# One queue for the first transfers of a decoder step, a shorter TensorE warm-up, and GpSimd on part of the last multiply

## The chip, the cores and the metric

The kernel runs on one core of one Trainium2 chip. The metric is the device time of one execution in microseconds (us). The kernel before was timed in three runs on the chip, and one further execution was taken with the hardware profiler. A core has five engines that run their own instruction streams: TensorE (PE, matrix multiply, with its weight loads shown apart as PEld), VectorE (DVE), ScalarE (ACT), GpSimd (POOL) and SyncE (SP). Transfers between memory and the core are issued by SP or by ACT (shown as SPq and ACTq) and carried out by 16 DMA engines.

## The reference

It is one inference step of one layer of a hybrid decoder, on 256 prompt tokens and 8 single-token samples (T = 264 columns, model width 2048):

```python
x = x + FFN_RES * swiglu(rmsnorm(x, n1), f1g, f1u, f1d)
h = rmsnorm(x, nm)
proj = h @ w_in
o_att, k_buf, v_buf = attend(q, k, v, sinks)
o_rwkv, shift, S = rwkv_time_mix(proj[..., ATT_COLS:], ...)
x = x + mixed @ w_out
x = x + FFN_RES * swiglu(rmsnorm(x, n2), f2g, f2u, f2d)
...
y = rmsnorm(x, final_norm)
```

where `swiglu(x, wg, wu, wd) = (silu(x @ wg) * (x @ wu)) @ wd` with an inner width of 5504 and `rmsnorm` divides by the root of the mean square and multiplies by a weight per feature. All values are float32.

## The kernel before

**Layout.** Features lie on the 128 partitions, tokens along the free dimension. The activations x are 16 tiles of 128 x 264 (`KD` = 16, `T` = 264). Each product keeps float32 accuracy by splitting both operands into a high part, rounded to the type TensorE reads, and a low part, the rest. Three matmuls are then run for each pair of 128 x 128 weight block and x tile: high by high, high by low, low by high (lines 140 to 142).

**Weights.** They are never kept. `chunk` (line 116) loads four 128 x 128 blocks (256 KB, 128 x 512) into one of six `raw` buffers by a transfer on SP, ACT casts them into one of four `hi` buffers, and VectorE (or GpSimd) subtracts to get one of four `lo` buffers. `gemm` (line 129) then runs the twelve matmuls of the chunk into a PSUM bank.

**The start.** `body` lets TensorE multiply a tile of ones by itself `NWARM` times (line 157), with no use for the result. `first_ffn` (line 280) issues, all on ACT, the transfer of `vec` (156 columns of norm weights and other vectors for the whole kernel) and six transfers of x. `ffn` (line 209) begins with a first phase over the eight PSUM banks: `load` splits the first four x tiles, then for every group of four x tiles (`k0` = 0, 4, 8, 12, the four rounds) it runs one chunk into each of the eight banks in turn, the gate and up halves of four column blocks. The x tiles of the next round are split while the last four banks of a round run. `Norm.split` (line 167) makes the parts of one x tile: ACT multiplies by the norm weight of that feature (taken from `vec`) and rounds to the high part, VectorE makes the low part. After the first phase the FFN goes on column block by column block. In its second part (`pi` = 1) `early` (line 197) issues the transfers of two more constants on ACT.

**The middle.** `mixing` holds attention and the recurrent half, as generators that are advanced between chunks of the projections. It is not touched.

**The end.** In `second_ffn` (line 899), `nxt` squares each finished x tile, and makes `ys`, that tile times its final norm weight. After the last tile the sums of squares go through small matmuls (lines 922 to 924) into a 88 x 3 tile `rt`. Five multiplies into `hot` (line 925), with no use for their result, are in TensorE's stream behind these. Meanwhile ACT and VectorE take the root and the reciprocal of `rt`, and three more small matmuls (line 931) spread the factors over all partitions into the PSUM bank `rp`. Seven multiplies on VectorE (line 933) scale the 16 output tiles in groups of 1, 1, 2, 4, 4, 2, 2, and each group leaves by a transfer issued on SP and ACT in turn.

**What sets the order.** Each engine works through a fixed stream. The framework orders the streams before the run by simulating a timeline (line 1041), so that an instruction stands where the simulation finds its operands ready. Instructions passed to `keep_in_program_order` stay in the order of the code. Waits between engines are added by the framework.

Of the kernel before, what the change touches and what calls it, by code (L numbers as in the profile page):

```python
# [7 lines left out]
F32 = mybir.dt.float32  # L8
F32R = mybir.dt.float32r
AF = mybir.ActivationFunctionType  # L10
ALU = mybir.AluOpType
AX = mybir.AxisListType

P = 128
NP = 256
NB = 8
T = NP + NB
D = 2048
KD = 16
# [8 lines left out]
CH, NRAW, NHL = 4, 6, 4  # L28
NACC, NM = 3, 5
NS, NO, NY, NH, NT, NLD = 38, 8, 8, 40, 18, 6  # L30
NWARM = 14
NGM, NKR, NUV, NTT, NBT = 10, 5, 3, 2, 5
NSTEP = 2
DWAIT = (8, 8, 8, 8)
# [7 lines left out]
VG1, VGM, VG2, VGF = 0, 16, 32, 48  # L42
# [5 lines left out]
def body(tc, I, O):  # L48
    nc = tc.nc
    V, A, G, TE, SP = nc.vector, nc.scalar, nc.gpsimd, nc.tensor, nc.sync  # L50
    cnt = [0]

    def uid(s):
        cnt[0] += 1
        return f"{s}{cnt[0]}"

    def tt(e, out, a, b, op):
        return e.tensor_tensor(out=out, in0=a, in1=b, op=op)  # L58

    def stt(out, a, s, b, op0, op1):  # L60
        return V.scalar_tensor_tensor(out=out, in0=a, scalar=s, in1=b, op0=op0, op1=op1)  # L61
# [5 lines left out]
    def act(out, in_, f, **k):  # L67
        return A.activation(out=out, in_=in_, func=f, **k)  # L68

    def bc(ap, shape):  # L70
        return ap.broadcast_to(list(shape))

    def mm(out, lhsT, rhs, start=True, stop=True, **k):
        TE.matmul(out, lhsT, rhs, start=start, stop=stop, **k)  # L74
# [20 lines left out]
    with ExitStack() as ctx:  # L95
        cp = ctx.enter_context(tc.tile_pool(name="cp", bufs=1))
        sp = ctx.enter_context(tc.tile_pool(name="sp", bufs=1))
        wp = ctx.enter_context(tc.tile_pool(name="wp", bufs=1))
# [4 lines left out]
        def slot(shape=(P, T), dt=F32, tag="s"):  # L103
            return sp.tile(list(shape), dt, tag=tag, bufs={"s": NS, "o": NO, "y": NY}[tag], name=uid(tag))
# [8 lines left out]
        def mp():  # L113
            return pp.tile([P, 512], F32, tag="m", bufs=NM, name=uid("m"))

        def chunk(src, n, e, ahead=True):
            w = n * P
            with tc.high_priority() if ahead else nullcontext():
                raw = wp.tile([P, CH * P], F32, tag="raw", bufs=NRAW, name=uid("raw"))
                hi = wp.tile([P, CH * P], F32R, tag="hi", bufs=NHL, name=uid("hi"))  # L120
                lo = wp.tile([P, CH * P], F32R, tag="lo", bufs=NHL, name=uid("lo"))
                SP.dma_start(raw[:, :w], src)  # L122
                A.copy(hi[:, :w], raw[:, :w])  # L123
                tt(e, lo[:, :w], raw[:, :w], hi[:, :w].bitcast(F32), ALU.subtract)
            return hi, lo

        nch = [0]

        def gemm(ps, src, xs, step=None, rng=None, ahead=True, share=False):
            n = len(xs)  # L130
# [15 lines left out]
        vec = cp.tile([P, NVEC], F32, name="vec")  # L146
# [9 lines left out]
        warm = mp()  # L156
        for _ in range(NWARM):
            mm(warm[:, :P], ones, ones)

        def vc(i):  # L160
            return vec[:, i:i + 1]

        class Norm:
            def __init__(self, col, most=2):
                self.col, self.most, self.xs, self.sums = col, most, [], [[], []]

            def split(self, x, pin=False, tag="s"):
                g = vc(self.col + len(self.xs))
                hi, lo = slot(dt=F32R, tag=tag), slot(dt=F32R, tag=tag)
                keep = tc.keep_in_program_order if pin else lambda i: i  # L170
                keep(act(hi, x, AF.Copy, scale=g))
                keep(stt(lo, x, g, hi.bitcast(F32), ALU.mult, ALU.subtract))
                self.xs.append((hi, lo))

# [22 lines left out]
        def early(pi):  # L197
            keep = tc.keep_in_program_order
            if pi == 1:
                keep(A.dma_start(C, I["cst"]))  # L200
                keep(A.dma_start(ss, I["shs"]))

# [6 lines left out]
        def ffn(nrm, xr, gu, dn, nxt, load, begin=False, side=None):  # L209
            rstd = None  # L210
            f0 = 0
            for pi, nf in enumerate(PARTS):
                hs = [None] * nf
                late = []
                if begin:
                    early(pi)
# [61 lines left out]
                f0 += nf  # L278

        def first_ffn(n2):  # L280
            n1 = Norm(VG1)
            xr = []
            A.dma_start(vec, I["vec"])
            def load(k0):
                n1.split(xr[k0], k0 >= CH)

            def nxt(o):
                n2.split(xr[o])
                n2.square(xr[o])
                A.dma_start(xsp[o], xr[o])  # L290

            with tc.tile_pool(name="f1", bufs=1) as fp:
                cur[0] = (fp, NH)
                for q in range(4):
                    xg = fp.tile([P, 4, T], F32, tag="x", bufs=4, name=uid("x"))
                    for j in ((0, 1), (1, 2), (2, 4)) if q == 0 else ((0, 4),):
                        A.dma_start(xg[:, j[0]:j[1]], I["xT"][:, q * 4 + j[0]:q * 4 + j[1], :])
                    xr += [xg[:, j] for j in range(4)]
                ffn(n1, xr, I["gu1"], I["dn1"], nxt, load, True)

        def dec_state(fp, XD):
# [33 lines left out]
        def mixing_body(mx, n2, n3, XD):  # L335
# [545 lines left out]
            for pi, ks in enumerate(PASS):  # L881
                now = need(ks)
                drain(now, [g for g in tasks if g not in now])
                with tc.high_priority():
                    for k in ks:
                        split(k)
                for o in range(KD):
                    ps = acc()
                    gemm(ps, I["wout"][o, :, k0 * P:(k0 + len(ks)) * P], [mixed[k] for k in ks], tick, share=True)
                    with tc.high_priority():  # L890
                        tt(V, xr[o], ps[:, :T], xr[o], ALU.add)
                    if pi == len(PASS) - 1 and o < CH:
                        n3.split(xr[o], tag="y")
                for k in ks:
                    mixed[k] = None
                k0 += len(ks)
            return xr

        def second_ffn(n3, xr, XD):
            fin = Norm(VGF, 3)  # L900

            def load(k):
                if k >= CH:
                    n3.split(xr[k], True, "o" if k in NSO else "s")

            with tc.tile_pool(name="f2", bufs=1) as fp:
                cur[0] = (fp, NH)
                ys = [fp.tile([P, 4, T], F32, tag="y", bufs=4, name=uid("y")) for _ in range(4)]
                rt = fp.tile([88, 8], F32, name="rt")

                def nxt(o):
                    fin.square(xr[o])
                    if o == 0:
                        act(rt[:, 7:8], fin.sums[0][0][0:88, 0:1], AF.Sqrt)
                    act(ys[o // 4][:, o % 4], xr[o], AF.Copy, scale=vc(VGF + o))

                side = dec_state(fp, XD)
                ffn(n3, xr, I["gu2"], I["dn2"], nxt, load, False, side)
                assert next(side, side) is side
                p = fin.sums[0]  # L920
                sm, rp, hot = [mp(), mp()], mp(), mp()
                for m, q in zip(sm, p):
                    for j in range(3):
                        mm(m[0:88, j:j + 1], q[:, j * 88:j * 88 + 88], ones[:, 0:1])
                for _ in range(5):
                    mm(hot[:, :P], ones, p[1][:, :P])
                A.copy(rt[:, 3:6], sm[0][0:88, 0:3])
                tt(V, rt[:, 0:3], sm[1][0:88, 0:3], rt[:, 3:6], ALU.add)
                act(rt[:, 0:3], rt[:, 0:3], AF.Sqrt, scale=1.0 / D, bias=eps[0:88, 0:1])
                V.reciprocal(rt[:, 0:3], rt[:, 0:3])  # L930
                for j in range(3):
                    mm(rp[:, j * 88:j * 88 + 88], bc(rt[:, j:j + 1], (88, P)), C[0:88, CID:CID + 88])
                for i, (o, n) in enumerate(((0, 1), (1, 1), (2, 2), (4, 4), (8, 4), (12, 2), (14, 2))):
                    y = ys[o // 4][:, o % 4:o % 4 + n]
                    tt(V, y, y, bc(rp[:, :T].unsqueeze(1), (P, n, T)), ALU.mult)
                    (SP, A)[i % 2].dma_start(O["yT"][:, o:o + n, :], y)

        xsp = [dp.tile([P, T], F32, tag=f"xsp{o}", name=f"xsp{o}") for o in range(KD)]
        n2, n3 = Norm(VGM), Norm(VG2)
        first_ffn(n2)  # L940
        with tc.tile_pool(name="dx", bufs=1) as dx:
            XD = dx.tile([P, 8, NPAIR, NB], F32, name="XD")
            second_ffn(n3, mixing(n2, n3, XD), XD)
# [29 lines left out]
def layout(i):  # L973
    c = np.ascontiguousarray
    f4 = np.float32
    a = {"xT": c(np.concatenate([i["x_prompt"][0].T, i["x_sample"][:, 0].T], 1).reshape(KD, P, T).transpose(1, 0, 2))}
    for n in (1, 2):
        f = lambda w: w.reshape(KD, P, NF, P).transpose(2, 1, 0, 3).reshape(NF, P, D)
        a[f"gu{n}"] = c(np.stack([f(i[f"ffn{n}_w_gate"][0]), f(i[f"ffn{n}_w_up"][0])], 1))
# [14 lines left out]
    s, t = np.arange(64)[:, None], np.arange(64)[None, :]  # L994
# [50 lines left out]
```

## Time and profile before

| | us |
|---|---|
| three timed runs | 2010.73, 2009.62, 2011.49 |
| median | 2010.73 |
| profiled execution | 2008.12 |
| span of the profiled execution, first to last instruction | 2006.0 |

The profile page gives for each engine the busy time, its share of the span and the number of instructions. Timelines list a start, a duration, the engine, the line of the kernel, the operation, output and input tiles with their shapes, a count of merged instructions, and in square brackets the idle time before the first of them and what ended it. Most operations stand in small helpers, so L58, L61, L68 and L74 are the lines of `tt`, `stt`, `act` and `mm`. A float32 matmul of `ones` is recorded as two passes. Groups list count, busy time, mean duration in ns, and the idle time before them with its releasers. Windows give, for each stretch of the span, its length, the busy time of PE, PEld, DVE, ACT and POOL with instruction counts, then the granted TensorE clock as a share of the full one, the DMA engines' busy share and GB/s.

### The profile page before, as it was taken

To read this page: it belongs to the slowest core of one execution; us is meant where nothing else is said; L and a number is where in the kernel's file an instruction comes from. 1 tells how busy PE (TensorE), PEld (TensorE's weight loads), DVE (VectorE), ACT (ScalarE), POOL (GpSimd) and SP (SyncE) were. 2 spreads that over 40 slices of the span, in tenths; PEclk is the share of its full clock that TensorE was granted. 3 is DMA by queue.
4 is the path that set the end of the run, shared out by engine and by line. 5 is a ranking of instruction groups with operands and counts; after the bars stand their busy time and mean duration, and the time that the engine had idled before them with its cause. 6 is when DMAs were issued, how large, how long until landed. Compare 5 with 4: busy or idle time off the path is not lost.

```text
span 2006.0 us, 45669 instructions
## 1 busy us (share of the span) xinstructions
PE 1980.9 (99%) x17126; PEld 1947.9 (97%) x17126; DVE 1300.9 (65%) x2550; ACT 1053.8 (53%) x2089; POOL 336.6 (17%) x433
## 2 busy tenths in 40 slices
PE   9999999999999999999999999999999999999998
PEld 9999999999999999998888899999999999999998
DVE  5865555655556577688768667765666666666665
ACT  5644444444444456766555655654444444444445
POOL 0401101010010122121123553120101001010012
PEclk9999999999999999999999999999999999999999
DMA  6566666655656567555555546565666666666654
GB/s 223 176 187 196 183 193 193 183 185 174 188 178 183 181 197 222 154 151 134 145 145 144 158 141 195 174 181 177 190 186 193 181 188 195 184 192 182 195 179 145
DMA packets 228798, 358.73 MB, mean 179 GB/s; under 512 B 42568, under 2 KB 83680, under 8 KB 228576
## 3 DMA queue, kind: packets, MB, share of 16 engines
q1 hardware_dynamic: 222112, 347.28, 57.9%
q10 hardware_dynamic: 6464, 8.54, 1.3%
q8 instruction: 134, 2.20, 0.5%
q14 instruction: 88, 0.72, 0.1%
HBM read 347.58 MB, written 10.22 MB: 178 GB/s over the span
## 4 chain that ended last, share of the span: by engine, by line
PE 92%; DVE 3%; DMA 2%; ACT 1%; issue 1%; SPq 1%; POOL 0%; DVEq 0%; ACTq 0%; POOLq 0%
PE acc L74 85%; PE m L74 7%; DVE lo L58 1%; DMA sb<-Xt 0%; DVE Xt L58 0%; DVE st L58 0%; DMA TT<-sb 0%; DMA raw<-in_win 0%; DMA raw<-in_gu 0%; ACT L68 0%; ACT hi L123 0%; DVE y L58 0%; SPq L122 0%; ACT t L68 0%; DMA Xt<-sa 0%
## 5 line engine op out<-in xcount | busy, mean ns | idle before, releaser
L123 ACT CAST hi<-raw 128x512 fp32r<-128x512 f32 (+2 forms) x1304 | 779.0, 602 | 827.5 <-PE acc L74 747.4
L58 DVE TENSOR_TENSOR lo<-raw,hi 128x512 fp32r<-128x512 f32 (+1 forms) x1248 | 853.4, 688 | 542.6 <-ACT hi L123 522.5
L74 PE MATMUL acc<-s,hi 128*128 128x264 f32 x5940 | 1108.9, 286 | 1.7 <-ACT hi L123 1.2
L74 PEld LDWEIGHTS acc<-s,hi 128*128 128x128 f32 x5940 | 921.9, 188 | 7.7 <-issue 1.8
L74 PE MATMUL acc<-s,lo 128*128 128x264 f32 x2970 | 846.9, 286 | 2.8 <-DVE lo L58 2.8
L74 PEld LDWEIGHTS acc<-s,lo 128*128 128x128 f32 x2970 | 558.9, 188 | 6.2 <-DVE lo L58 3.4
L74 PE MATMUL acc<-t,hi 128*128 128x264 f32 x2752 | 503.0, 285 | 0.0
L74 PEld LDWEIGHTS acc<-t,hi 128*128 128x128 f32 x2752 | 426.5, 188 | 0.0
L74 PE MATMUL acc<-t,lo 128*128 128x264 f32 x1376 | 389.1, 285 | 0.0
L58 POOL TENSOR_TENSOR t<-t,t 128x264 f32<-128x264 f32 (+1 forms) x148 | 150.5, 1017 | 1150.1 <-ACT hi L123 781.5
L74 PEld LDWEIGHTS acc<-t,lo 128*128 128x128 f32 x1376 | 258.5, 188 | 0.1
L74 PE MATMUL acc<-y,hi 128*128 128x264 f32 x648 | 124.5, 285 | 0.0
L74 PEld LDWEIGHTS acc<-y,hi 128*128 128x128 f32 x648 | 101.0, 188 | 0.2
L74 PE MATMUL acc<-y,lo 128*128 128x264 f32 x324 | 91.9, 284 | 0.0
L58 DVE TENSOR_TENSOR t<-acc,t 128x264 f32<-128x264 f32 x156 | 67.4, 432 | 36.5 <-PE acc L74 36.3
L58 POOL TENSOR_TENSOR lo<-raw,hi 128x512 fp32r<-128x512 f32 x56 | 73.2, 1309 | 69.5 <-ACT hi L123 45.8
L58 POOL TENSOR_TENSOR o<-o,o 128x264 f32<-128x264 f32 x43 | 36.1, 841 | 189.9 <-ACT o L68 184.2
L74 PE MATMUL acc<-o,hi 128*128 128x264 f32 x324 | 63.3, 285 | 0.0
L74 PEld LDWEIGHTS acc<-y,lo 128*128 128x128 f32 x324 | 60.9, 188 | 0.0
L61 DVE SCALAR_TENSOR_TENSOR s<-acc,s 128x264 f32<-128x264 f32 x96 | 40.6, 427 | 15.9 <-PE acc L74 15.5
L74 PEld LDWEIGHTS acc<-o,hi 128*128 128x128 f32 x324 | 50.3, 188 | 0.0
L74 PE MATMUL m<-s,hi 128*128 128x264 f32 x260 | 48.7, 286 | 0.0
(239 smaller groups left out, 1345.8 us busy)
## 6 DMA issues: line engine op xcount, KB each, us to landing
raw<-in_gu SPq DMA_DIRECT2D x688, 256.0 KB, 3.4
raw<-in_dn SPq DMA_DIRECT2D x224, 256.0 KB, 2.9
raw<-in_win SPq DMA_DIRECT2D x152, 256.0 KB, 3.5
raw<-in_dn SPq DMA_DIRECT2D x160, 192.0 KB, 2.8
raw<-in_wout SPq DMA_DIRECT2D x48, 256.0 KB, 3.3
raw<-in_wout SPq DMA_DIRECT2D x32, 128.0 KB, 3.0
xsp<-x ACTq DMA_DIRECT2D x16, 132.0 KB, 3.5
s<-xsp SPq DMA_DIRECT2D x16, 132.0 KB, 4.5
```

Source lines behind the costliest of these rows:

```text
L58: return e.tensor_tensor(out=out, in0=a, in1=b, op=op)
L61: return V.scalar_tensor_tensor(out=out, in0=a, scalar=s, in1=b, op0=op0, op1=op1)
L74: TE.matmul(out, lhsT, rhs, start=start, stop=stop, **k)
L123: A.copy(hi[:, :w], raw[:, :w])
```

## The change

- The first transfers are issued on SP in one list with fixed order: the first x tile, w0 (the first chunk of weights), then x1, x2-3, w1, w2, x4-7, w3, x8-11, w4, x12-15, w5. The weights go into the buffers that the first six calls of `chunk` would have taken (`pre`), and these calls issue no transfer. ACT issues none of them.
- The 16 columns of the first norm's weights are appended to the first x tile in memory (`layout`) and on the core (`x0`, 280 columns), and `Norm` reads them there (`gain`). The transfer of `vec` moves to `early(1)`.
- The high part of x0 is made by VectorE (`ts`, a tensor_scalar multiply) instead of ACT.
- `NWARM` goes from 14 to 10, the `hot` multiplies from 5 to 4.
- The factors are also copied from PSUM into `rs` by ACT. The 16 output tiles are multiplied in ten instructions: VectorE keeps tiles 0 to 11 as 1, 1, 2, 4, 2, 2, and GpSimd multiplies tiles 12, 13, 14 and 15 one by one, reading `rs`. With the order of the list, the transfers of the GpSimd tiles and of tile 1 are issued on ACT, the others on SP.

```diff
-NWARM = 14
+NWARM = 10
...
-                raw = wp.tile([P, CH * P], F32, tag="raw", bufs=NRAW, name=uid("raw"))
+                raw = pre.pop(0) if pre else None
+                ready = raw is not None
+                if not ready:
+                    raw = wp.tile([P, CH * P], F32, tag="raw", bufs=NRAW, name=uid("raw"))
...
-                SP.dma_start(raw[:, :w], src)
+                if not ready:
+                    SP.dma_start(raw[:, :w], src)
...
-            def split(self, x, pin=False, tag="s"):
-                g = vc(self.col + len(self.xs))
+                self.gain = gain
+
+            def split(self, x, pin=False, tag="s", e=None):
+                k = len(self.xs)
+                g = vc(self.col + k) if self.gain is None else self.gain[:, k:k + 1]
...
-                keep(act(hi, x, AF.Copy, scale=g))
+                if e is None:
+                    keep(act(hi, x, AF.Copy, scale=g))
+                else:
+                    ts(e, hi, x, g, ALU.mult)
...
             if pi == 1:
+                keep(A.dma_start(vec, I["vec"]))
                 keep(A.dma_start(C, I["cst"]))
...
-            n1 = Norm(VG1)
             xr = []
-            A.dma_start(vec, I["vec"])
+
             def load(k0):
-                n1.split(xr[k0], k0 >= CH)
+                n1.split(xr[k0], k0 >= CH, e=None if k0 else V)
...
-                for q in range(4):
-                    xg = fp.tile([P, 4, T], F32, tag="x", bufs=4, name=uid("x"))
-                    for j in ((0, 1), (1, 2), (2, 4)) if q == 0 else ((0, 4),):
-                        A.dma_start(xg[:, j[0]:j[1]], I["xT"][:, q * 4 + j[0]:q * 4 + j[1], :])
-                    xr += [xg[:, j] for j in range(4)]
+                keep = tc.keep_in_program_order
+
+                def weights(i):
+                    raw = wp.tile([P, CH * P], F32, tag="raw", bufs=NRAW, name=uid("raw"))
+                    keep(SP.dma_start(raw, I["gu1"][i // 2, i % 2][:, :CH * P]))
+                    pre.append(raw)
+
+                x0 = fp.tile([P, T + KD], F32, name="x0")
+                keep(SP.dma_start(x0, I["xT"][:, :T + KD]))
+                n1 = Norm(VG1, gain=x0[:, T:])
+                xr.append(x0[:, :T])
+                weights(0)
+                for i, n in enumerate((1, 2, 4, 4, 4)):
+                    xg = fp.tile([P, n, T], F32, name=f"xg{i}")
+                    k = KD + len(xr) * T
+                    keep(SP.dma_start(xg.rearrange("p k t -> p (k t)"), I["xT"][:, k:k + n * T]))
+                    xr += [xg[:, j] for j in range(n)]
+                    for j in ((), (1, 2), (3,), (4,), (5,))[i]:
+                        weights(j)
...
-                for _ in range(5):
+                for _ in range(4):
                     mm(hot[:, :P], ones, p[1][:, :P])
...
-                for i, (o, n) in enumerate(((0, 1), (1, 1), (2, 2), (4, 4), (8, 4), (12, 2), (14, 2))):
+                rs = fp.tile([P, T], F32, name="rs")
+                A.copy(rs, rp[:, :T])
+                for i, (o, n) in enumerate(((0, 1), (1, 1), (2, 2), (12, 1), (4, 4), (13, 1), (8, 2), (14, 1), (10, 2), (15, 1))):
                     y = ys[o // 4][:, o % 4:o % 4 + n]
-                    tt(V, y, y, bc(rp[:, :T].unsqueeze(1), (P, n, T)), ALU.mult)
+                    e, r = (V, rp[:, :T]) if o < 12 else (G, rs)
+                    tt(e, y, y, bc(r.unsqueeze(1), (P, n, T)), ALU.mult)
                     (SP, A)[i % 2].dma_start(O["yT"][:, o:o + n, :], y)
...
-    a = {"xT": c(np.concatenate([i["x_prompt"][0].T, i["x_sample"][:, 0].T], 1).reshape(KD, P, T).transpose(1, 0, 2))}
+    x = np.concatenate([i["x_prompt"][0].T, i["x_sample"][:, 0].T], 1).reshape(KD, P, T).transpose(1, 0, 2)
+    a = {"xT": c(np.concatenate([x[:, 0], i["ffn1_norm"][0].reshape(KD, P).T, x[:, 1:].reshape(P, -1)], 1))}
```

More of the change, by code (lines that the diff above doesn't have):

```diff
@@ L125, in chunk @@
             return hi, lo
-        nch = [0]
+        nch, pre = [0], []
         def gemm(ps, src, xs, step=None, rng=None, ahead=True, share=False):
@@ L163, in body, with __init__ @@
         class Norm:
-            def __init__(self, col, most=2):
+            def __init__(self, col, most=2, gain=None):
                 self.col, self.most, self.xs, self.sums = col, most, [], [[], []]
-            def split(self, x, pin=False, tag="s"):
-                g = vc(self.col + len(self.xs))
+                self.gain = gain
+            def split(self, x, pin=False, tag="s", e=None):
+                k = len(self.xs)
+                g = vc(self.col + k) if self.gain is None else self.gain[:, k:k + 1]
                 hi, lo = slot(dt=F32R, tag=tag), slot(dt=F32R, tag=tag)
                 keep = tc.keep_in_program_order if pin else lambda i: i
-                keep(act(hi, x, AF.Copy, scale=g))
+                if e is None:
+                    keep(act(hi, x, AF.Copy, scale=g))
+                else:
+                    ts(e, hi, x, g, ALU.mult)
                 keep(stt(lo, x, g, hi.bitcast(F32), ALU.mult, ALU.subtract))
```

## The prediction

> **What bounds the kernel now.** First the page's first part: TensorE works almost the whole span, so time can only be won where it waits or runs slowly.
>
> ```profile
> PE 1980.9 (99%) x17126; PEld 1947.9 (97%) x17126; DVE 1300.9 (65%) x2550; ACT 1053.8 (53%) x2089; POOL 336.6 (17%) x433
> ```
>
> The change touches only the two ends, so I read the timeline of the first 10 us next (start, duration, engine, line, operation).
>
> ```profile
> 0.71 0.42 ACTq L283 DMA_DIRECT2D vec<-in_vec  x1
> ...
> 0.72 9.32 SPq L122 DMA_DIRECT2D raw<-in_gu  x8
> ...
> 0.97 6.23 PE L74 MATMUL m<-ones 128*128 128x128 f32 x28 [0.97 <-POOL eps L153]
> ...
> 1.23 1.35 ACTq L297 DMA_DIRECT2D x<-in_xT  x3
> ...
> 4.92 2.35 ACTq L297 DMA_DIRECT2D x<-in_xT  x3
> 7.33 0.52 ACT L68 ACTIVATE s<-x,vec 128x264 fp32r<-128x264 f32 x1 [4.66 <-DMA raw<-in_gu]
> ...
> 8.40 1.04 PE L74 MATMUL acc<-s,hi 128*128 128x264 f32 x4 [1.20 <-ACT hi L123]
> ```
>
> ACT issues vec and three x transfers by 2.6 us, then stands still until 4.92. Only after its seventh issue, at 7.33, does it start on x0. The real matmuls begin at 8.40, 1.20 us after the warm-up ends. The landing times (KB each, us from issue to landing) explain the stop:
>
> ```profile
> raw<-in_gu SPq DMA_DIRECT2D x1, 256.0 KB, 4.2
> ...
> x<-in_xT ACTq DMA_DIRECT2D x1, 132.0 KB, 4.8
> ```
>
> The first weight tile w0 was issued at 0.72 and landed at 4.92, the very moment ACT issues again. Four issues on each queue were then out: the ninth waits for a landing. x0, issued at 1.23, landed at 6.03, but ACT was behind its remaining issues until 7.28, as the chain of waits says:
>
> ```profile
> 1.62 5.30 DMA raw<-in_gu
> 6.92 0.02 issue
> 6.94 0.33 ACTq L297
> ...
> 23.34 4.24 PE acc L74 x35
> ...
> 34.85 4.36 PE acc L74 x36
> ...
> 46.47 4.36 PE acc L74 x36
> ```
>
> The first phase is four rounds over eight PSUM banks, 12 matmuls a bank. A round starts with the acc banks: rounds two, three and four begin at 23.34, 34.85 and 46.47. An undisturbed round thus takes 46.47 - 34.85 = 11.62 us, 1.45 a bank, 0.121 a matmul. The first takes 23.34 - 8.40 = 14.94, so **3.32 us are lost inside round one**. The busy times by stretch show why (engines, then granted clock, DMA share, GB/s):
>
> ```profile
> 0.00:4.00 4.00, 3.03 (x14) 3.03 (x15) 0.00 (x0) 1.49 (x2) 0.46 (x7) 1.00 0.45 104
> 4.00:5.00 1.00, 1.00 (x7) 1.00 (x7) 0.00 (x0) 0.00 (x0) 0.00 (x0) 1.00 1.06 357
> 5.00:8.00 3.00, 2.21 (x11) 2.01 (x10) 0.12 (x1) 0.67 (x2) 0.00 (x0) 1.00 1.04 399
> 8.00:10.00 2.00, 1.59 (x9) 1.23 (x9) 1.99 (x4) 2.00 (x5) 0.00 (x0) 1.00 1.01 355
> 10.00:11.00 1.00, 1.00 (x6) 0.93 (x6) 1.00 (x3) 1.00 (x3) 0.00 (x0) 0.68 0.98 339
> 11.00:13.00 2.00, 2.00 (x11) 2.00 (x11) 1.09 (x3) 0.14 (x1) 0.00 (x0) 0.50 1.01 379
> 13.00:14.00 1.00, 1.00 (x7) 1.00 (x7) 0.00 (x0) 0.00 (x0) 0.00 (x0) 0.61 1.02 396
> ```
>
> The granted clock is half from 10.36 (0.68 in that slice) to 13.78 (0.61): 3.42 us, which cost half, 1.71. The other 1.6 us went to operands arriving one by one and a late cast. The warm-up too was at half speed, whatever the column says for it: 6.23 / 28 = 0.22 us a pass, against 1.36 / 10 = 0.14 for the same shape in the row of 1995.00 below.
>
> **The change, the start.** All early transfers go out on SP: x0 with the norm weights (143 KB), w0, x1, x2-3, w1, w2, x4-7, w3, x8-11, w4, x12-15, w5. ACT issues none, so its 4.66 us wait ends when w0 lands. Eight issues at the 0.44 us spacing of SP (9.32 us hold two stops, the first four came by 2.5) are out by 4.2; the ninth waits for x0, which lands by about then.
>
> *When w0 lands.* x0 and w0 are 405 KB. By 4.0 the old kernel's engines had moved 104 GB/s x 4 us = 0.42 MB, so 4.0 is the early end. The late end is w0's own landing, 4.92, plus 143 KB ahead of it at 357 GB/s, 0.4: 5.3. Landings lag the bytes, so I take 4.9. The first matmul follows after the cast and semaphores:
>
> ```profile
> L58 DVE TENSOR_TENSOR lo<-raw,hi 128x512 fp32r<-128x512 f32 x12 | 7.8, 686 | 5.8 <-ACT hi L123 5.8
> L123 ACT CAST hi<-raw 128x512 fp32r<-128x512 f32 x12 | 6.9, 615 | 6.5 <-PE acc L74 4.8 <-PE m L74 0.9 <-DVE lo L58 0.8
> L61 DVE SCALAR_TENSOR_TENSOR s<-x,vec,s 128x264 fp32r<-128x264 f32 x8 | 3.6, 487 | 7.9 <-ACT s L68 7.9
> ```
>
> 4.9 + 0.6 = **5.5** (4.65 to 5.9 from the bounds). The shorter warm-up, 20 of 28 passes x 0.2225 us, ends at 0.97 + 4.45 = 5.42 and so lets it start; 5.42 replaces the early end. Fourteen would have held TensorE to 7.2. The x0 split on DVE is a multiply that the trace does not show; between zero and the 0.49 us of its neighbour, either fits before w0's landing; uncovered it costs 0.49. Start: 8.40 - 5.5 = **2.9 us won**.
>
> *What is late next.* x1 and x2-3 land about 5.3 and 6.0 (0.54 and 0.81 MB by the same rates and 0.9 lag). DVE then owes one low part (0.69) and three x remainders (0.49 each), done near 7.7, so bank 0 ends about 8.0. Its 2.5 us instead of 1.45 contain the half clock and 0.3 for feeding. If the clock changes in steps as long as the one stretch seen (an estimate from those rows), a step lies at 10.36 - 3.42 = 6.94, so 1.45 us run at half: 0.7. Banks 1 to 3 have their weights in time. By 13.0 the engines have moved 0.42 + 0.36 + 1.20 + 0.71 + 0.34 + 0.76 = 3.78 MB; w5 ends the first 3.75 MB, lands near 13.5, and its low part is done at 14.8 where TensorE wants it at 14.3: 0.5 lost. 0.55 I reserve for the planner's order of these instructions. Together 2.05 instead of 3.32: **1.3 us won**. Bounds for this loss: 0.7 (clock alone) and 3.3 (as now). Rounds two to four had no idle and keep none.
>
> *The moved vec* is one ACT issue, 0.42 us, in the second part of the FFN, where ACT is half idle and the first reader of vec comes at that FFN's end: nothing, and 0.42 without cover. The old wait goes away, none is added behind it.
>
> [...]
>
> **The change, the end.** These rows carry it:
>
> ```profile
> 1995.00 1.36 PE L74 MATMUL m<-o,ones 128*128 128x128 f32 x10
> 1996.20 0.80 PE L74 MATMUL m<-C,rt 88*128 88x88 f32 x6
> ...
> 1995.77 0.17 DVE L930 RECIPROCAL rt<-rt 88x3 f32<-88x3 f32 x1 [0.36 <-ACT rt L68]
> 1997.04 4.94 DVE L58 TENSOR_TENSOR y<-y,m 128x264 f32<-128x264 f32 x7 [1.10 <-PE m L74]
> ```
>
> ```profile
> L58 DVE TENSOR_TENSOR y<-y,m 128x1056 f32<-128x1056 f32 x2 | 2.4, 1247 | 0.0
> L58 DVE TENSOR_TENSOR y<-y,m 128x528 f32<-128x528 f32 x3 | 2.0, 697 | 0.0
> ...
> L58 POOL TENSOR_TENSOR o<-o,o 128x264 f32<-128x264 f32 x14 | 11.3, 806 | 37.4 <-ACT o L68 31.7 <-PE acc L74 4.0 <-issue 1.7
> L58 POOL TENSOR_TENSOR t<-t,t 128x264 f32<-128x264 f32 x4 | 4.5, 1132 | 36.1 <-DVE t L58 18.2 <-ACT hi L123 18.0
> ...
> L232 ACT COPY t<-m x6: 358/366/372, 52.7 to 1283.8; 128x264 f32<-128x264 f32 x6
> ```
>
> ```profile
> 1998.30:2000.00 1.70, 0.00 (x0) 0.00 (x0) 1.70 (x3) 0.00 (x0) 0.00 (x0) 1.00 0.85 314
> 2000.00:2000.50 0.50, 0.00 (x0) 0.00 (x0) 0.50 (x1) 0.00 (x0) 0.00 (x0) 0.84 0.19 72
> 2000.50:2004.60 4.10, 0.00 (x0) 0.00 (x0) 1.48 (x3) 0.00 (x0) 0.00 (x0) 0.50 1.00 387
> ```
>
> One hot multiply less removes two passes, 0.27 us, but the reciprocal ends at 1995.94 while the next group starts at 1996.20: 0.0 to 0.26, I take **0.1**.
>
> VectorE loses four of sixteen columns: one 1056-wide multiply (1.25) becomes 528-wide (0.70), one 528-wide goes, so 4.94 becomes about 3.75. GpSimd gets a copy of the factors (0.37 on ACT, which has only issues left to do) and four multiplies at 0.81 (0.75 to 1.13): done 0.45 + 3.2 = 3.7 after the factors. But the transfers end this stage: they are saturated from 2000.5 to 2004.6. I replayed the issues, 0.85 us to first bytes, 400 KB a us: the old order ends 7.5 us after 1997.04 (trace: 7.56). The new one, with pieces from GpSimd at 1.3, 2.1, 2.9 and 3.7 filling the dips before 2000.5, ends at 6.9: **0.6 us won**. With 1.13 us multiplies the last piece is out at 5.0 and still waits for the queue: same end. Bounds: 0, if smaller pieces lower the rate by a tenth, and 1.1, if no dip is left.
>
> Sum: 2.9 + 1.3 + 0.1 + 0.6 = **4.9 us**. The profiled execution took 2008.12 (span 2006.0 and 2.1 around it), so 2003.2 by its own measure. The three timed runs have a median of 2010.73, 2.6 above it; I take the gain from that: **2005.8**.
>
> **Rivals.** *The clock comes late or is lost again.* [...] Another 3.42 us at half costs 1.7: gain 3.2, 2007.5.
>
> *The one queue brings weights too late.* For: w4 and w5 stand behind 1.08 MB of x. Against: the engines moved 355 to 399 GB/s with two queues, and nothing here says one gives less. If the landings slip by 1 us, banks 4 and 5 wait 1.5 more: gain 3.4, 2007.3.
>
> *A kinder phase.* If the warm-up gets its full clock before 5.5, 0.7 of cold matmuls go and GpSimd's best end adds 0.5: gain 6.1, 2004.6.
>
> *The planner re-sorts the mixing stage.* The order of all engines comes from its simulated timeline, and earlier starts there shift every later tie. TensorE's waits between 24 and 1990 us include
>
> ```profile
> PE m L74 <- ACT t L68: 4.0, 4, 1.6
> ...
> PE m L448 <- DVE S L61: 1.8, 1, 1.8
> ```
>
> Four more waits of 1.6 us, 6.4, would take the gain: 1.5 slower, 2012.2. It decides from three such waits on (4.8). Against: after 60 us everything is TensorE paced and shifts together.
>
> **Chances.** Forecast 0.60, clock 0.15, late weights 0.08, kinder phase 0.09, planner 0.08. The forecast's own unknowns put the gain between 3.3 and 5.9. 0.2% is 4.0 us, about what a measurement of this kernel can tell from no change. The forecast lies beyond it in 8 of 10 (0.49), the kinder phase always (0.09), clock and late weights in one of five (0.05): faster 0.63. Slower by 4.0 needs six extra waits, half of the planner's chance: 0.04. Within: 0.33. The range holds kinder phase, clock and late weights: 2004.4 to 2009.0.
>
> **What would show it.** Right: SP's queue first in the timeline with ACT idle of issues; x0's split before w0's cast; first real matmul at 5.4 to 5.9; round two at 19.2 instead of 23.34; no half clock after 7; factors copied to rs, the last transfer about 0.6 us earlier after the factors. Wrong: a first matmul after 6.5, a stretch of clock 0.5 behind 8 us, bank 4 or 5 waiting over 1 us, or waits between 24 and 1990 us that grew by microseconds.

## The result and the profile after

The changed kernel takes 2002.3 us in the median of six runs (1998.84 to 2005.45). The kernel before, in six runs as well, takes 2009.2 (2007.83 to 2011.49). The ratio is 0.996, with a 95% interval of [0.9949, 0.9972] (given in brackets below too): faster by 6.9 us, where 4.9 and 2005.8 were forecast. The time lies 2.1 us below the low end of the range. The profiled execution of the changed kernel took 2002.93 (span 2001.1).

First the page's engine line. TensorE is busy for as long as before, so again it is its waits that have to be compared.

```profile
PE 1980.3 (99%) x17116; PEld 1945.5 (97%) x17116; DVE 1304.9 (65%) x2550; ACT 1055.0 (53%) x2089; POOL 340.3 (17%) x437
```

The timeline of the first 10 us and ACT's timeline up to 24 us, of the changed kernel:

```profile
0.97 4.63 PE L74 MATMUL m<-ones 128*128 128x128 f32 x20 [0.97 <-POOL eps L157]
2.88 0.36 DVE L65 TENSOR_SCALAR s<-x 128x264 fp32r<-128x264 f32 x1 [2.88 <-DMA x<-in_xT]
5.00 0.62 ACT L127 CAST hi<-raw 128x512 fp32r<-128x512 f32 x1 [2.78 <-DMA raw<-in_gu]
5.67 0.81 PE L74 MATMUL acc<-s,hi 128*128 128x264 f32 x2
...
8.68 0.62 ACT L127 CAST hi<-raw 128x512 fp32r<-128x512 f32 x1 [0.35 <-DMA raw<-in_gu]
10.73 0.62 ACT L127 CAST hi<-raw 128x512 fp32r<-128x512 f32 x1 [1.43 <-DMA raw<-in_gu]
12.78 0.62 ACT L127 CAST hi<-raw 128x512 fp32r<-128x512 f32 x1 [1.43 <-DMA raw<-in_gu]
14.83 0.62 ACT L127 CAST hi<-raw 128x512 fp32r<-128x512 f32 x1 [1.01 <-DMA raw<-in_gu]
```

x0 is multiplied by VectorE at 2.88, the first weights are cast at 5.00, the first real matmul runs at 5.67 instead of 8.40: **2.73 us won** at the first matmul. Then the casts of w2 to w5 follow 2.05 us apart, each released by its own transfer. The chain of waits says what that does to round one:

```profile
6.67 8.06 DMA raw<-in_gu
...
14.83 0.63 ACT hi L127
...
15.48 0.70 DVE lo L58
...
16.23 4.41 PE m L74 x34
20.64 4.36 PE acc L74 x36
...
32.28 4.36 PE acc L74 x36
```

w5 lands at 6.67 + 8.06 = 14.73. Its low part is done at 16.18, and only then do the last three banks run, 4.41 us. At full pace from 5.67 on they would have started at 5.67 + 5 x 1.45 = 12.92. So this wait would cost 3.31 us by itself, had nothing before it been late. Round one loses 20.64 - 5.67 - 11.62 = 3.35; before, it lost 3.32.

TensorE is behind long before w5, though. Its timeline has 14 matmuls from the first one at 5.67 up to this row:

```profile
9.35 0.51 PE L74 MATMUL acc<-s,hi 128*128 128x264 f32 x2 [0.21 <-ACT hi L127]
```

They take 3.68 us, and 14 x 0.121 = 1.69 at full pace: 2.0 us are gone while x1, w1 and w2 arrive (w1 is cast at 7.71, w2 at 8.68); a half clock, shown below, has a share in it. The waits for the low parts of w4 and w5, which end at 14.18 and 16.23, take 0.33 and 0.49 more. The two readings overlap: a late w5 alone would lose nearly all of it, and an early w5 alone could win back little over 1 us. The start as a whole has won 23.34 - 20.64 = **2.7 us**. The windows give a granted clock of 1.00 all the way, with the DMA engines busy all the time:

```profile
5.00:8.00 3.00, 2.94 (x11) 1.98 (x11) 1.96 (x4) 2.34 (x5) 0.00 (x0) 1.00 0.93 330
8.00:10.00 2.00, 1.79 (x12) 1.39 (x12) 1.49 (x3) 0.95 (x2) 0.00 (x0) 1.00 1.02 332
10.00:11.00 1.00, 1.00 (x10) 1.00 (x10) 0.03 (x1) 0.27 (x1) 0.00 (x0) 1.00 1.02 395
11.00:13.00 2.00, 2.00 (x18) 2.00 (x17) 0.69 (x1) 0.57 (x2) 0.00 (x0) 1.00 1.04 416
```

For the first matmuls the column says too much, as it did for the warm-up before. In the kernel before a weight load takes 0.33 us inside the stretch of half clock and 0.19 from 13.80 on, behind it. Two of TensorE's weight loads in the changed kernel:

```profile
6.39 0.29 PEld L74 LDWEIGHTS acc<-s,lo 128*128 128x128 f32 x1 [0.23 <-DVE lo L58]
...
7.16 0.19 PEld L74 LDWEIGHTS acc<-s,hi 128*128 128x128 f32 x1 [0.24 <-DVE s L61]
```

By these lengths, 0.29 us and 0.19, the real matmuls began at half clock and had the full one by 7.16.

The end is a timeline again:

```profile
1988.42 0.56 PE L74 MATMUL m<-ones,o 128*88 128x1 f32 x6
...
1991.10 0.90 PE L74 MATMUL m<-C,rt 88*128 88x88 f32 x6
1992.04 0.38 ACT L957 COPY rs<-m 128x264 f32<-128x264 f32 x1 [1.20 <-PE m L74]
1992.45 3.77 DVE L58 TENSOR_TENSOR y<-y,m 128x264 f32<-128x264 f32 x6 [1.40 <-ACT rs L957]
1992.50 2.84 POOL L58 TENSOR_TENSOR y<-y,rs 128x264 f32<-128x264 f32 x4 [4.60 <-ACT rs L957]
```

The kernel before has the first of these rows at 1993.31:

```profile
1993.31 0.56 PE L74 MATMUL m<-ones,o 128*88 128x1 f32 x6
```

From that row to the end of the span it is 2001.1 - 1988.42 = 12.68 after and 2006.0 - 1993.31 = 12.69 before: the new end wins **nothing**. The factors come 0.21 earlier after the row (2.68 against 2.89), the multiplies and transfers take 8.65 instead of 8.96, but VectorE's first multiply, which started 0.84 after the factor matmuls, starts 1.35 after them, released by ACT's copy to `rs`.

So 2.7 of the span's 4.9 us come from the start and none from the end. The other 2.2 lie in between, in code that the change does not touch. TensorE's busy time in the recurrent part of the middle, windows of the kernel before and of the changed one:

```profile
720.00:1260.00 540.00, 526.92 (x5225) 496.17 (x5224) 397.86 (x1010) 338.10 (x809) 161.14 (x250) 1.00 0.56 162
```

```profile
720.00:1260.00 540.00, 530.54 (x5234) 498.95 (x5233) 403.77 (x1012) 339.99 (x811) 162.06 (x250) 1.00 0.56 163
```

In these 540 us TensorE stands still for 13.1 us before and 9.5 after. The waits are other ones too. After:

```profile
PE m L74 <- ACT t L68: 3.3, 2, 2.2
...
PE m L74 <- DVE y L61: 1.5, 1, 1.5
PE m L74 <- DVE N L58: 1.1, 1, 1.1
```

Those on y and N are new, and others (on st and uv) have gone or shrunk. That is not the same stream run earlier; it is another order. In the compiled instruction streams, with the tile numbers left out, some 900 of the mixing stage's rows stand in another place than before. The profile shows 2.2 us for it; the experiments below put a number on it over many runs.

### The profile page after: what moved, and what is told of

Read it like the earlier page. It is cut to its first block, busy times and chain, and to the rows that moved or that the text cites. A ratio compares the mean times of both kernels' runs of the same rounds, so it can differ in the third digit from the quotient of the medians.

```text
span 2001.1 us, 45661 instructions
## 1 busy us (share of the span) xinstructions
PE 1980.3 (99%) x17116; PEld 1945.5 (97%) x17116; DVE 1304.9 (65%) x2550; ACT 1055.0 (53%) x2089; POOL 340.3 (17%) x437
## 4 chain that ended last, share of the span: by engine, by line
PE 94%; DVE 3%; DMA 2%; SPq 1%; ACT 0%; issue 0%; POOL 0%; DVEq 0%; POOLq 0%; ACTq 0%
PE acc L74 86%; PE m L74 7%; DVE lo L58 0%; DVE Xt L58 0%; DMA Xt<-sa 0%; DMA raw<-in_gu 0%; DVE st L58 0%; DMA xg<-in_xT 0%; SPq L126 0%; DVE y L58 0%; PE m L523 0%; DVE t L703 0%; ACT hi L127 0%; DMA TT<-sb 0%; SPq L555 0%
```

## The experiments

Twelve runs on three chips: the first four shared the runs of the kernel before (median 2009.98), so did the next four (2010.76), and the last four (2010.40). The compiled streams of each variant show which of two orders its mixing stage has, and small edits at the start flip it: "old" below is the order of the kernel before, "new" that of the changed one. The traces agree: with the tile numbers left out, at least 104 of VectorE's instructions between 60 and 1980 us stand elsewhere than in the kernel before in every profile called new, at most 17 in every one called old. In the table, "round two" is the start of round two, "waits" is 540 less TensorE's busy time from 720 to 1260, "middle" goes from round two to the last copy of an acc bank in the first phase of the second FFN, and "end" goes from the first sum matmul to the end of the span; each from the profile of that run.

| run | order | round two | waits | middle | end | timed median, ratio to before |
|---|---|---|---|---|---|---|
| before | old | 23.34 | 13.1 | 1252.8 | 12.69 | |
| after | new | 20.64 | 9.5 | 1251.6 | 12.68 | 2002.30, 0.996 [0.9949, 0.9972] |
| e1_after_again | new | 20.68 | 9.3 | 1252.4 | 12.73 | 2002.69, 0.9963 [0.995, 0.9975] |
| e2_vec_start | old | 20.43 | 13.8 | 1253.4 | 12.73 | 2006.35, 0.9981 [0.9973, 0.999] |
| e3_weights_first | old | 19.68 | 14.9 | 1257.6 | 12.69 | 2007.61, 0.9982 [0.9973, 0.9991] |
| e4_tail_only | old | 23.09 | 15.6 | 1255.6 | 12.67 | 2009.93, 0.9997 [0.9988, 1.0006] |
| e5_before_new_order | new | 25.09 | 10.1 | 1252.6 | 12.80 | 2007.71, 0.9986 [0.9977, 0.9995] |
| e6_w4_early | new | 20.52 | 8.3 | 1250.3 | 12.68 | 2003.57, 0.9968 [0.9958, 0.9978] |
| e7_two_banks | new | 21.00 | 10.4 | 1254.0 | 12.42 | 2003.80, 0.9968 [0.9955, 0.998] |
| e8_warm14 | new | 21.08 | 9.8 | 1251.6 | 12.72 | 2003.77, 0.9968 [0.9956, 0.9979] |
| e9_weights_ahead | new | 19.41 | 9.1 | 1250.0 | 12.70 | 2001.68, 0.9956 [0.9944, 0.9969] |
| e10_ahead_two_banks | new | 19.23 | 10.7 | 1253.4 | 12.41 | 2003.50, 0.9966 [0.9952, 0.9979] |
| e11_before_warm10 | old | 22.30 | 14.6 | 1256.0 | 12.71 | 2008.90, 0.9995 [0.9986, 1.0003] |
| e12_after_third | new | 20.50 | 7.9 | 1249.7 | 12.66 | 2002.51, 0.9957 [0.9944, 0.9969] |

### Is it the order of the mixing stage?

**e1**: the changed kernel again, with no edit.

> The changed kernel once more, without any edit, for a second profile and a ratio on the chip of its neighbours. Theory P (the start gives 2.7 us, the planner's new order of the mixing stage the rest, the end nothing): faster than before by 4.5 to 7 us; in the profile TensorE's waits between 720 and 1260 us sum to 8.5 to 10.5 us again, round two starts within 0.5 us of 20.6. Theory R (the mixing stage differs only by scatter between executions): the same total, but the waits between 720 and 1260 us may come out anywhere from 8 to 14.

2002.69, 7.3 us below the 2009.98 of before on that chip. The waits are 9.3 again: the shorter middle belongs to the kernel, not to one execution.

**e2**: the new start and end, but `vec` stays at the start, issued on ACT, which brings the old order back.

```diff
-                keep(A.dma_start(vec, I["vec"]))
...
+                A.dma_start(vec, I["vec"])
                 ffn(n1, xr, I["gu1"], I["dn1"], nxt, load, True)
```

> The changed kernel with one edit: the transfer of vec is issued on ACT at the start again. The first tiles still come on SP and the end is the changed one; but the planner's order of the mixing stage is then that of the kernel before in all but 27 rows (the changed kernel differs from it in some 900). Theory P: the start's 2.7 us stay (2.2 to 2.9, vec takes 78 KB of the first transfers) and the mixing stage's gain goes: 2 to 3.5 us faster than before, 3 to 4 slower than the changed kernel; waits between 720 and 1260 us near 13. Theory R: as the changed kernel within 1 us, 4.5 to 7 faster than before.

Round two starts at 20.43, a little earlier than in the changed kernel, and the end takes the same 12.73 as in e1. Yet it takes 2006.35, 3.7 us more than e1. The window and the waits of e2 between 720 and 1260:

```profile
720.00:1260.00 540.00, 526.24 (x5218) 495.27 (x5217) 398.15 (x1010) 337.40 (x809) 162.90 (x250) 1.00 0.57 162
```

```profile
PE m L74 <- ACT t L68: 3.6, 4, 1.4
PE m L74 <- DVE st L58: 1.7, 2, 1.2
PE m L74 <- ACT uv L621: 1.4, 1, 1.4
```

13.8 us of waits, with those on st and uv back and none on y or N. What the new start and end win by themselves is 2009.98 - 2006.35 = 3.6.

**e5** is the other direction: the kernel before with its own start and end, but the last three transfers of x cut in two, which gives the new order.

```diff
-                    for j in ((0, 1), (1, 2), (2, 4)) if q == 0 else ((0, 4),):
+                    for j in ((0, 1), (1, 2), (2, 4)) if q == 0 else ((0, 2), (2, 4)):
```

> The kernel before, with its start, its ACT queue and its end, and one edit: the last three x transfers are split in two. The planner then gives the mixing stage the order of the changed kernel in all but 8 rows. Theory P (the order is worth a few microseconds by itself): TensorE's waits between 720 and 1260 us sum to 8.5 to 10.5 us as in the changed kernel instead of 13 to 15.6, the last FFN takes 716.2 instead of 717.2 us, and the total is 2 to 5 us faster than before less what three more issues on ACT cost the start (0 to 2.5 us, read from the start of round two, 23.3 before). Theory R: waits of 13 to 15 and no gain, or a loss by the start.

The start gets worse: round two begins at 25.09 instead of 23.34. Still the kernel is 3.05 us faster by the medians (2007.71 against 2010.76) and 2.8 by the ratio. Its window and waits:

```profile
720.00:1260.00 540.00, 529.91 (x5226) 498.22 (x5225) 402.14 (x1012) 338.50 (x810) 162.08 (x250) 1.00 0.57 162
```

```profile
PE m L74 <- ACT t L68: 2.4, 2, 1.9
PE m L74 <- DVE y L61: 1.3, 1, 1.3
PE m L74 <- DVE N L58: 1.1, 1, 1.1
```

The waits on y and N, 10.1 in all, come with the order and without anything else of the change. With the 1.75 that the start gives away, the order is worth 2.8 + 1.75 = 4.6.

Over all profiles the waits of the two groups do not overlap: the old order waits 13.1 to 15.6 us (mean of five 14.4), the new one 7.9 to 10.7 (mean of nine 9.5). The middle as a whole does overlap (1252.8 to 1257.6 against 1249.7 to 1254.0); in the mean it takes 1255.1 against 1251.7, 3.4 less, and the second FFN's stretch from there to its first sum matmul is 1.0 shorter in every profile with the new order (716.2 or 716.3 against 717.2 or 717.3). Together **4.4 us**, between the 3.7 and the 4.6 of the two timed comparisons. The one profile of before on which the prediction was built has the shortest middle of the old order, which is why the profiles show 2.2 where the timed runs show about 4.

### The start

**e3**: w3 moves ahead of x4-7, w4 and w5 ahead of x8-11.

```diff
-                    for j in ((), (1, 2), (3,), (4,), (5,))[i]:
+                    for j in ((), (1, 2, 3), (4, 5), (), ())[i]:
```

> The changed kernel with the SP list reordered: x2-3, w1, w2, w3, x4-7, w4, w5, x8-11, x12-15. The late-weights theory (round one now loses its 3.3 us to chunks that stand behind 1.08 MB of x): round two starts 1.5 to 2.5 us earlier than 20.6, at 18.1 to 19.1, and casts 4 to 6 no longer stand 2.05 us apart. The order theory (round one loses its time to the planner's order of TensorE, whatever lands): round two stays within 0.5 us of 20.6. The mixing stage has the order of before here in all but 22 rows: by theory P the total is 4 to 5.5 us faster than before, by theory R 6 to 9.

Round two moves from 20.64 to 19.68, less than the 1.5 to 2.5 us expected. Now it is w6, issued behind x8-15 because its transfer is not in the list, whose cast comes late:

```profile
15.35 0.62 ACT L127 CAST hi<-raw 128x512 fp32r<-128x512 f32 x1 [2.06 <-DMA raw<-in_gu]
```

The total does not gain from it, since this edit falls into the old order (waits 14.9, middle 1257.6): 2007.61, 2.4 below before where 4 to 5.5 were expected.

**e6**: w3 and w4 earlier, w5 still last.

```diff
-                    for j in ((), (1, 2), (3,), (4,), (5,))[i]:
+                    for j in ((), (1, 2, 3), (4,), (), (5,))[i]:
```

> The changed kernel with the SP list x0, w0, x1, x2-3, w1, w2, w3, x4-7, w4, x8-11, x12-15, w5; the mixing stage keeps the order of the changed kernel. Late-weights theory: w3 is cast about 1.3 us and w4 about 1.3 us earlier than in the changed kernel, w5 to w7 at the same times or 0.3 later, because the same 3.75 MB stand before them; round two starts 0 to 0.7 us earlier than 20.6 and the total is that of the changed kernel within 1 us, 6 to 8 us faster than before. Order theory: round two moves by more than 1 us.

Round two at 20.52, which is within the 20.50 to 20.68 of the unedited kernel. As long as w5 is last, the cast that follows it stays where it was:

```profile
14.71 0.62 ACT L127 CAST hi<-raw 128x512 fp32r<-128x512 f32 x1 [2.36 <-DMA raw<-in_gu]
```

**e9**: all eight chunks of round one ahead of x8 to x15; w6 and w7 wait for buffers of the first chunks.

```diff
-                    for j in ((), (1, 2), (3,), (4,), (5,))[i]:
+                    for j in ((), (1, 2, 3), (4, 5, 6, 7), (), ())[i]:
```

> The changed kernel with all eight weight chunks of round one (w6 and w7 too) ahead of x8-11 and x12-15 in the SP list; the mixing stage keeps the order of the changed kernel in all but 8 rows. Late-weights theory: w5 stands behind 2.66 MB instead of 3.75, so its cast moves from 14.8 to 12 or 12.5, round one is then set by TensorE, and round two starts at 18.2 to 19.2 instead of 20.6; the total is 1.4 to 2.4 us faster than the changed kernel. Order theory (round one's 3.3 us lie in the order of TensorE): round two no earlier than 20.0.

The casts now follow one another with no transfer in between after 11.58, and round two and three start 1.1 to 1.3 us earlier than in the three profiles of the changed kernel (chain of waits):

```profile
11.58 0.62 ACT L127 CAST hi<-raw 128x512 fp32r<-128x512 f32 x1 [1.46 <-DMA raw<-in_gu]
12.53 0.61 ACT L127 CAST hi<-raw 128x512 fp32r<-128x512 f32 x1
```

```profile
19.41 3.14 PE acc L74 x26
...
31.02 4.36 PE acc L74 x36
```

So the late weights were worth 1.1 to 1.3 us, and x8 to x15 can come later at no cost seen here. That is less than expected (round two at 18.2 to 19.2): round one still loses 19.41 - 5.95 - 11.62 = 1.84 us behind a first matmul at 5.95. Most of it is lost at once, as in the changed kernel; 14 matmuls come before this row of TensorE's timeline:

```profile
9.12 0.51 PE L74 MATMUL acc<-s,hi 128*128 128x264 f32 x2
```

They take 3.17 us instead of 1.69, so 1.5 us go to the arrival of the first operands, which this edit does not move. In time it is 2001.68 against 2002.51 for the unchanged kernel on the same chip (e12): the fastest version tried and the shortest profiled span (1998.3), but the intervals of the two ratios overlap nearly whole, so this is not a shown gain.

**e8**: `NWARM` 14 in the changed kernel.

```diff
-NWARM = 10
+NWARM = 14
```

> The changed kernel with a warm-up of 14 instead of 10. If TensorE is what the first real matmul waits for, it moves from 5.7 to 7.3 or, with the clock raised before the warm-up ends, to 6.5; if the weights set round one (late-weights theory), round two still starts within 0.4 us of 20.6 and the total is that of the changed kernel within 1 us. If the shorter warm-up is what was won, round two starts 0.8 to 1.6 us later.

First real matmul at 6.03, round two at 21.08. Neither is due to the longer warm-up. It ended at 0.97 + 4.94 = 5.91, since its 28 passes took 0.18 us each in the mean and not the 0.2225 that gave the prediction its 7.2, and the first matmul waited for the cast of w0 (ACT's and PEld's timelines):

```profile
5.36 0.62 ACT L127 CAST hi<-raw 128x512 fp32r<-128x512 f32 x1 [3.15 <-DMA raw<-in_gu]
6.03 0.30 PEld L74 LDWEIGHTS acc<-s,hi 128*128 128x128 f32 x2 [0.30 <-ACT hi L127]
```

6.03 lies within the 5.67 to 6.16 of the changed kernel's three profiles. Round two is 0.4 to 0.6 later than theirs because TensorE waits for the low part of w5 until 16.66 here. The timed medians do not separate ten from fourteen either (2003.77 against 2003.57 and 2003.80 of e6 and e7, on the same chip). So a gain by the shorter warm-up is not shown; no profile with the new start has 28 passes as slow as the 6.23 us of before.

**e11**: `NWARM` 10 in the kernel before.

```diff
-NWARM = 14
+NWARM = 10
```

> The kernel before with a warm-up of 10 and nothing else; its mixing order does not move. If the first real matmul waits for ACT and the transfers, as read from the profile: it stays at 8.4, the idle stretch before it grows from 1.2 to about 3 us, and the total is within 0.5 us of before, or up to 1.7 us slower if the clock is lost for one window more. If the warm-up was what held the start: up to 1.8 us faster.

Ratio 0.9995 [0.9986, 1.0003]. TensorE only stands still longer, since there ACT's issues set the start (timeline):

```profile
8.12 1.11 PE L74 MATMUL acc<-s,hi 128*128 128x264 f32 x4 [2.51 <-ACT hi L123]
```

Round two starts at 22.30 in this profile, 0.8 to 1.0 earlier than in the two others with that start (23.34 before, 23.09 in e4); the time does not show it.

### The end

**e4**: the kernel before with the changed end alone.

```diff
-                for _ in range(5):
+                for _ in range(4):
...
+                rs = fp.tile([P, T], F32, name="rs")
+                A.copy(rs, rp[:, :T])
...
-                    tt(V, y, y, bc(rp[:, :T].unsqueeze(1), (P, n, T)), ALU.mult)
+                    e, r = (V, rp[:, :T]) if o < 12 else (G, rs)
+                    tt(e, y, y, bc(r.unsqueeze(1), (P, n, T)), ALU.mult)
```

> The kernel before with the end of the changed one (four hot multiplies, factors copied to rs, GpSimd on four tiles); start and mixing stage are ordered as before. My reading of the profile after (VectorE's first multiply waits 0.4 us for the copy to rs, which eats the 0.2 us of the hot multiply and the fuller transfers): no change within 0.5 us, and from the last sum matmuls to the end of the span 11.5 us as before. The prediction's own sum: 0.7 us faster. A loss through smaller pieces: 0.5 to 1 us slower.

Ratio 0.9997 [0.9988, 1.0006], end 12.67: nothing, in time as in the profile.

**e7**: the factors are spread a second time, into a PSUM bank of their own, from which ACT copies.

```diff
-                A.copy(rs, rp[:, :T])
+                rq = mp()
+                for j in range(3):
+                    mm(rq[:, j * 88:j * 88 + 88], bc(rt[:, j:j + 1], (88, P)), C[0:88, CID:CID + 88])
+                A.copy(rs, rq[:, :T])
```

> The changed kernel with three more small matmuls that put the factors into a second PSUM bank, from which ACT copies them to rs. Theory W (VectorE's first multiply waits for ACT because both read the same bank; VectorE is the one that starts the transfers): VectorE starts 0.35 to 0.45 us earlier after the sum matmuls, 2.45 us instead of 2.83, and the span ends 0.3 to 0.6 us earlier after them (12.1 to 12.4 instead of 12.68 us from the first sum matmul). Theory D (the transfers alone set the end, whenever VectorE starts): no change of the end within 0.1 us. The median is too coarse for this; the profile decides.

The timeline of its end:

```profile
1993.96 1.57 PE L74 MATMUL m<-C,rt 88*128 88x88 f32 x12
1994.90 3.78 DVE L58 TENSOR_TENSOR y<-y,m 128x264 f32<-128x264 f32 x6 [0.99 <-PE m L74]
...
1995.57 0.38 ACT L960 COPY rs<-m 128x264 f32<-128x264 f32 x1 [1.87 <-PE m L74]
```

VectorE is now released by TensorE, 0.94 after the factor matmuls began instead of 1.35, and ACT's copy runs beside it. The end takes 12.42, 0.26 less than in the changed kernel and 0.27 less than before. So the wait came with the shared bank; e10 repeats it (0.94 and 12.41). With one bank VectorE stands behind the copy (1.35), with two it doesn't (0.94). Whether the hardware needs that order or only the framework sets it is not shown: no run here lets both read one bank together.

A gain of 0.26 cannot be seen in the timed runs (2003.80).

**e10**: e9 and e7 together.

```diff
-                    for j in ((), (1, 2), (3,), (4,), (5,))[i]:
+                    for j in ((), (1, 2, 3), (4, 5, 6, 7), (), ())[i]:
...
+                rq = mp()
...
-                A.copy(rs, rp[:, :T])
+                A.copy(rs, rq[:, :T])
```

> The same with the factors in two PSUM banks as well, as the version that should beat both kernels: the start of the run before, the end 0.25 us shorter than the changed kernel's; 8 to 10 us faster than the kernel before.

Round two at 19.23 and an end of 12.41, the best of both in one profile. The time, 2003.50, is 6.9 below before where 8 to 10 were expected, and not better than e9's or e12's: the some 1.5 us that this profile wins at both ends against e12's are less than what the middle scatters (1253.4 here, 1249.7 there, in the same order).

**e12**: the changed kernel a third time, as the measure for e9 and e10.

> The changed kernel once more, beside the two versions above on one chip: 6 to 8 us faster than before, waits between 720 and 1260 us of 8.5 to 10.5 us.

2002.51, 7.9 below before on that chip. With 2002.3 and 2002.69 the changed kernel agrees within 0.4 us on all three.

## Why the prediction was wrong, step by step

**The start: right up to the first matmul, then wrong in size.** The first matmul was forecast at 5.5 and ran at 5.67 (5.83, 5.95 and 6.16 in e1, e9 and e12, which issue the same first transfers). The half clock was forecast up to 6.94, for 0.7 us; the weight loads confirm it up to about 7, but its cost cannot be told from the waits for x1 in the same stretch, and no half clock follows in that profile. Two terms failed. The sum gave the first bank 1.0 us of loss (0.7 and 0.3) and had the weights of banks 1 to 3 in time; 2.0 us were gone by 9.35, with w1 and w2 cast only at 7.71 and 8.68. And w5 was to land at 13.5 and landed at 14.73, its low part done at 16.18 where 14.8 was forecast. The bytes came more slowly than the two queues of before had shown: 286 GB/s from 4 to 5 us and 330 and 332 from 5 to 10, where 357, 399 and 355 had been summed up. By 13.0 that makes 3.59 MB instead of 3.78, half a microsecond. The other 0.7 lies between the bytes and the landing, some 1.3 us where the sum has 0.6; why is open. So "late weights", given 0.08 as a rival, is a part of what happened inside round one: e9 wins 1.1 to 1.3 by moving them, and e6 shows that nothing short of moving w5 helps. The predicted 1.3 us in round one became 0.0, and the start 2.7 instead of 4.2.

**The end: wrong in size.** Forecast 0.7, measured 0.0, twice. The multiplies got as short as forecast (3.77 us for 3.75) and GpSimd's four took 2.84 for 3.2. What was missed is that the copy to `rs` was set beside VectorE's first multiply, while both read the bank `rp`: the copy stands in front of that multiply, which starts 1.35 us after the factor matmuls instead of 0.84. And the output transfers gained 0.3 where 0.6 was forecast.

**The middle: the step that decides.** The prediction gave the planner's re-sorting a chance of 0.08, only to the slower side, and put against it that after 60 us everything is TensorE paced and shifts together. The re-sorting is what happened, and to the faster side: e2 takes it away and loses 3.7, e5 has it alone and gains 4.6 less its own late start. That sentence was the error: TensorE waited 9.5 us in the mean from 720 to 1260 instead of 14.4. The planner places each instruction by a simulated time. The likely reading is that a shift at the start decides between two candidates nearly equal and a whole stage then falls into another order; which tie flipped was not traced. There was no reason in the profile for a sign, so an effect of several us on either side belonged into the range.

**The base.** The forecast was counted from 2010.73, the median of three runs. Six gave 2009.2. Of the 3.5 us between forecast and measurement, 1.5 are this, and 2.0 are the gain: 4.2 + 0.7 + 0 = 4.9 forecast, 2.7 + 0.0 + 4.4 = 7.1 measured, against the 6.9 to 7.9 of the timed comparisons. That the two profiled spans also differ by 4.9 is chance, since the profile of before has a lucky middle.

**Still open**: why the new order waits less. The lists show which waits come and go, but not by which single move of an instruction.

## What to carry to other kernels

Where a planner orders the instruction streams, an edit at one end is not local: compare the compiled order of the far stages before costing them at nothing, and test the order by itself with a neutral edit that flips it. Where many transfers share one queue in order of need, look at the last operand of the first round and at the first ones: here the late weights were worth 1.1 to 1.3 us and the arrival of the first operands 1.5. Count each landing from the rate of the first microseconds (286 to 332 GB/s from 4 to 10 us here), and put operands of later rounds behind them. Where a helper copies out of a PSUM bank that another engine is about to read, look which of the two is set first: here the copy stood in front of VectorE, whose first multiply came 1.35 us after the factor matmuls, and 0.94 after them once the copy had a bank of its own.

## What the runs showed of the hardware that was not expected

**A half clock that costs almost nothing.** In e7, which has the same start as the changed kernel, the granted clock is half from about 8.8 to 12.2 us:

```profile
10.00:12.00 2.00, 2.00 (x11) 2.00 (x10) 0.70 (x2) 0.62 (x1) 0.00 (x0) 0.50 1.02 409
```

Round two then starts at 21.00, only 0.36 later than in the changed kernel's own profile; a like stretch in e12, from 7.6 to 11.0, leaves it at 20.50. The time that TensorE loses to the clock is mostly time it would have spent waiting for w4 and w5: in these two profiles its timeline has no such wait left, and the chain of waits up to round two is TensorE alone from 8.68 on in e7 and from 6.89 in e12. The clock rival of the prediction thus did occur in some executions, without its price of 1.7.

**One stretch of half clock in the middle.** In the changed kernel's profile (windows of 2 us) TensorE is busy for 0.52 of the 2 us from 1028, and then:

```profile
1030.00:1032.00 2.00, 2.00 (x19) 1.82 (x20) 1.86 (x6) 0.26 (x1) 0.00 (x0) 0.74 0.13 37
1032.00:1034.00 2.00, 2.00 (x11) 2.00 (x11) 0.70 (x2) 0.67 (x3) 0.00 (x0) 0.50 0.85 223
1034.00:1036.00 2.00, 2.00 (x16) 1.78 (x15) 1.37 (x3) 1.14 (x4) 0.85 (x2) 0.91 0.44 113
```

The half clock lasts 1.04 + 2.00 + 0.36 = 3.4 us and costs at most half of it, 1.7. Eight of the nine profiles with the new order have such a stretch between 1020 and 1040 us, and two of the five with the old one; the shortest span (e9) has none. The length is that of the stretch at the start of the kernel before, 3.42 us. What brings it on is not shown: in the 3.41 us ahead of it, from 1027.55 to 1030.96, TensorE is busy for 1.93 us. How much the stretch adds to the 6.6 us between the fastest and the slowest timed run of this kernel was not tested.
